# Key preparation in a two-layer attention trunk: layer 0's rotation sums and norm products on VectorE, and the low parts of the keys in one VectorE instruction

## The chip, the cores and the metric

The kernel runs on one core of one Trainium2 chip. The time is the device time of one execution in microseconds (us). In the profile PE is TensorE (matmuls and transposes), PEld its weight loads, DVE is VectorE, ACT is ScalarE, POOL is GpSimd and SP is SyncE, which issues all the large DMAs here.

## The reference, cut to what matters

Two layers act on `x` of 256 tokens by 1024 features. Layer 0 is an attention with 16 query heads in 4 groups: each head attends to compressed keys, to selected blocks of keys (with 256 tokens all blocks are selected) and to a window of keys; three gates mix the results. Layer 1 is a sliding-window attention with 2 key heads and a sink. Both multiply the result with `silu(z)` and project it back.

```python
q = q_groups(rope(rms_norm(split_heads(q, N_HEADS), q_gain), positions), g)
k_slc = kv_groups(rope(rms_norm(split_heads(ks, g), k_gain[1]), positions))   # layer 0
k_win = kv_groups(rope(rms_norm(split_heads(kw, g), k_gain[2]), positions))   # layer 0
k     = kv_groups(rope(rms_norm(split_heads(k, g), k_gain), positions))       # layer 1
```

What matters here is how these keys come about: a head's 64 values are divided by their root mean square, multiplied by a gain, and rotated (`x1*cos - x2*sin`, `x2*cos + x1*sin`).

## The kernel before, in words

All products run in float32 pieces: a value is split into a high part (float32r) and a low part, and a product is made from high times high, high times low and low times high. So each weight tile goes through a copy that rounds it (`wh`, line 141 on ACT, line 143 on DVE) and a subtraction (`wl`, line 169 on DVE) before its matmuls (line 114). Each weight tile's matmuls with `wl` are a third of the tile's matmuls: for a tile of two blocks of 128 rows and both halves of the tokens that is 4 of 12.

The tokens are worked on in two halves of 128 (`h` is 0 or 1), one token per partition. Keys are prepared by `k_prep`, which is called three times: for the window keys of layer 0 (accumulator `akw`), for the selected keys of layer 0 (`aks`), both with 4 key heads (`ng` = 4, so 256 values per token), and for layer 1's keys (`akv`, `ng` = 2, 128 values per token). For each half a call does the following.

- ACT squares the projection (line 310), and DVE sums the squares per head (`kssq`, line 311).
- DVE makes the two rotation terms `t1` and `t2` out of the accumulator (lines 323 and 324); in the trace both are called `rt`.
- POOL turns the sums of squares of both halves into `kr`, one scaling and one power of -0.5.
- POOL adds the rotation terms (`rt<-rt,rt`) and multiplies by the norm (`rt<-rt,kr`).
- ACT writes the high part of the key twice, side by side (`kp<-rt`, line 376).
- The low part is the difference of `t1` and the high part. It is needed twice too: DVE makes copy 0 (line 382), and POOL makes copy 1 (`kp<-rt,kp`, line 66).
- PE transposes the high and the low part (`ptk`, line 385) and ACT copies each to `kt` (line 386).

Every instruction of POOL goes through a small helper class, so POOL's tensor-tensor instructions all stand at line 66 and its tensor-scalar ones at line 71. The tile names tell them apart. `kp` shares its two buffers with `qs`, the split queries, and `ptk` takes one of two PSUM buffers that all transposes share.

The steps of layer 0 are written in the order: window keys, compression (`ph`, `hx`, `kcm`, and on POOL `cssq` and `cr`), selected keys, then queries `q0`, gate `z0`, attention `a0`, queries `q1` and so on. This is not the order in which the instructions run. The framework orders each engine's instructions while it builds the program, by priorities (`tc.high_priority`; `k_prep` has an offset of 250) and by a planner that simulates the engines' times (line 905, `schedule_with_timeline_sim=True`). The result is one fixed list per engine, each worked off in its order. A change of an instruction's engine or size can therefore change the order of others.

The queries of layer 0 (`aq`) use the same accumulators for both of their halves of heads; `q_prep` does for queries what `k_prep` does for keys, with the sum of the rotation terms on POOL (128x512) and the low part on DVE (line 263). The gate `z` is accumulated in a PSUM tile `pz` of which there is one buffer, freed by a DVE product (`zt`, line 400).

Of the kernel before, what the change touches and what calls it, by code (L numbers as in the profile page):

```python
# [20 lines left out]
F32 = mybir.dt.float32  # L21
# [4 lines left out]
ALU = mybir.AluOpType  # L26
# [5 lines left out]
HD = 64  # L32
# [9 lines left out]
PSC1 = 'pp'  # L42
PSL = 'pppd'
SQE = 'aaaa'
RSK, KLO = 'p', 'dp'
OZH, QHI, KHI = 'a', 'a', 'a'
KTM = 'pd'
ZE = 'dp'
OZL, RTE, SSE = 'd', 'p', 'd'
# [41 lines left out]
def tile_hybrid_trunk(ctx: ExitStack, tc: tile.TileContext, x, positions, norm_gains, a_w_in, a_cmp_pos,  # L91
                      a_cmp_w2, a_w_out, b_w_in, b_w_out, small, cmp_w1, out):
    nc = tc.nc
    pool = Pool(nc.gpsimd)
    ENG = {'d': nc.vector, 'p': pool}
# [212 lines left out]
    def sumsq(dst, ps, n, r):  # L308
        sq = work.tile([128, n, HD], F32, name="sq", tag="sq", bufs=1)
        nc.scalar.activation(sq, ps, AF.Square, scale=r)  # L310
        ENG[SSE].tensor_reduce(dst, sq, axis=AX.X, op=ALU.add)

    def rope_terms(ps, n, h, tab, eng='d'):

        t1 = work.tile([128, n, HD], F32, name="rt1", tag="rt1")
        t2 = work.tile([128, n, HD], F32, name="rt2", tag="rt2")
        if tab is None:
            c = trig0[:, h, 2, None, None, :].to_broadcast([128, n, 2, 32])
            s = trig0[:, h, None, 0:2, :].to_broadcast([128, n, 2, 32])
        else:  # L320
            c = halves(tabc[:, h, tab:tab + 1]).to_broadcast([128, n, 2, 32])
            s = halves(tabs[:, h, tab:tab + 1]).to_broadcast([128, n, 2, 32])
        nc.vector.tensor_tensor(halves(t1), halves(ps), c, op=ALU.mult)
        ENG[eng].tensor_tensor(halves(t2), swap_halves(ps, n), s, op=ALU.mult)  # L324
        return t1, t2

    def dup(ap, n):
        return ap[:, :, None, :].to_broadcast([128, n, 2, HD])
# [28 lines left out]
    def k_prep(pss, ng, tab, kt, c0, rf):  # L357

        with tc.high_priority(offset=HPK):
            ssq = work.tile([128, 2, ng], F32, name="kssq", tag="kssq")  # L360
            r = work.tile([128, 2, ng], F32, name="kr", tag="kr")
            for h in range(2):
                sumsq(ssq[:, h], pss[h], ng, rf[:, h:h + 1])
            ts = [rope_terms(pss[h], ng, h, tab, 'd') for h in range(2)]
            pool.tensor_scalar(ssq, ssq, 1.0 / HD, EPS, op0=ALU.mult, op1=ALU.add)
            pool.tensor_tensor(r, ssq, mhalf[:, :, None].to_broadcast([128, 2, ng]), op=ALU.pow)
            for h in range(2):
                t1, t2 = ts[h]
                ENG[RTE].tensor_tensor(t1, t1, t2, op=ALU.add)
                ENG[RSK].tensor_tensor(t1, t1, r[:, h, :, None].to_broadcast([128, ng, HD]), op=ALU.mult)  # L370
                kp = work.tile([128, 2, ng, 2, HD], F32R, name="kp", tag="qs", bufs=NQS)
                for part in range(2):
                    ks = kp[:, part]
                    if part == 0:
                        if KHI == 'a':
                            nc.scalar.activation(ks, dup(t1, ng), AF.Copy)
                        else:
                            for a in range(2):
                                ENG[KHI].tensor_copy(ks[:, :, a], t1)
                    else:  # L380
                        for a in range(2):
                            ENG[KLO[a]].tensor_tensor(ks[:, :, a], t1, kp[:, 0, :, a].bitcast(F32), op=ALU.subtract)
                    pt = ps_t.tile([128, ng, 128], F32R, name="ptk", tag="pt")
                    for g in range(ng):
                        nc.tensor.transpose(pt[:, g], ks[:, g].rearrange("p a d -> p (a d)"), identr)
                    nc.scalar.activation(kt[:, part, :, c0[h]:c0[h] + 128], pt, AF.Copy)
# [200 lines left out]
    with tc.tile_pool(name="cmp", bufs=1) as cp:  # L587
# [20 lines left out]
        for h in range(2):  # L608
# [3 lines left out]
            t1, t2 = rope_terms(kc, 4, h, None, 'd')  # L612
# [18 lines left out]
        def keys_selected():  # L631

            acc = banks("aks", "s")
            for kk in range(4):
                w = load_w(awi, 2 * kk, 2, 1536, 512)
                for h in range(2):
                    proj(acc[h], hT, h, w, 2, 2 * kk)
            k_prep([heads(acc[h][:, 0:256]) for h in range(2)], 4, 2, kt, K_SLC, r0)
            for h in range(2):
                nc.scalar.activation(vv[:, 0, h], acc[h][:, 256:512].rearrange("p (g d) -> p g d", d=HD), AF.Copy,  # L640
                                     scale=r0[:, h:h + 1])

        def keys_window():
            acck = banks("akw")
            for k0 in (0, 4):
                w = load_w(awi, k0, 4, 2048, 256)
                for h in range(2):
                    proj(acck[h][:, 0:256], hT, h, w, 4, k0)
            accv = banks("avw", "s")
            for k0, nk in ((0, 3), (3, 3), (6, 2)):  # L650
                w = load_w(awi, k0, nk, 2304, 304)
                for h in range(2):
                    proj(accv[h][:, 0:304], hT, h, w, nk, k0)
            k_prep([heads(acck[h][:, 0:256]) for h in range(2)], 4, 3, kt, K_WIN, r0)
            for h in range(2):
                nc.scalar.activation(vv[:, 1, h], accv[h][:, 0:256].rearrange("p (g d) -> p g d", d=HD), AF.Copy,
                                     scale=r0[:, h:h + 1])
                gt = work.tile([128, 48], F32, name="gt", tag="gt", bufs=1)
                nc.scalar.activation(gt, accv[h][:, 256:304], AF.Tanh, scale=r0h[:, h:h + 1])
                nc.vector.tensor_scalar(gate[:, h].rearrange("p a b -> p (a b)"), gt, 0.5, 0.5, op0=ALU.mult, op1=ALU.add)  # L660
            nc.vector.tensor_scalar(gate[:, 0, 0, :], gate[:, 0, 0, :], valid, None, op0=ALU.mult)
# [159 lines left out]
    def keys1():  # L821
        acc = banks("akv1", "s")
        wk = [load_w(bwi, k0, 4, 1024, 256) for k0 in (0, 4)]
        for kk in range(2):
            for h in range(2):
                proj(acc[h][:, 0:256], hT, h, wk[kk], 4, 4 * kk)
        k_prep([heads(acc[h][:, 0:128]) for h in range(2)], 2, 5, kt1, (0, 128), r1)
        for h in range(2):
            nc.scalar.activation(v1[:, h], heads(acc[h][:, 128:256]), AF.Copy, scale=r1[:, h:h + 1])
# [79 lines left out]
```

## Time and profile before

| | |
|---|---|
| median of 3 runs | 289.76 us |
| lowest and highest | 289.17 and 291.66 us |
| the profiled execution, its own time | 289.89 us |
| its span, first to last instruction | 288.1 us |
| mean granted TensorE clock | 0.987 of full speed |

The profiled execution's own time is 1.8 us above its span, and 0.13 us above the median. Busy times of an engine are sums over its instructions; instructions of one engine overlap by some hundredths to tenths of a us, so that a row of several together can be shorter than their sum.

### The profile page before, as it was taken

To read this page: it belongs to the slowest core of one execution; us is meant where nothing else is said; L and a number is where in the kernel's file an instruction comes from. 1 tells how busy PE (TensorE), PEld (TensorE's weight loads), DVE (VectorE), ACT (ScalarE), POOL (GpSimd) and SP (SyncE) were. 2 spreads that over 40 slices of the span, in tenths; PEclk is the share of its full clock that TensorE was granted. 3 is DMA by queue.
4 is the path that set the end of the run, shared out by engine and by line. 5 is a ranking of instruction groups with operands and counts; after the bars stand their busy time and mean duration, and the time that the engine had idled before them with its cause. 6 is when DMAs were issued, how large, how long until landed. Compare 5 with 4: busy or idle time off the path is not lost.

```text
span 288.1 us, 5292 instructions
## 1 busy us (share of the span) xinstructions
PE 271.3 (94%) x1772; PEld 229.1 (80%) x1772; DVE 221.1 (77%) x621; ACT 184.2 (64%) x441; POOL 124.3 (43%) x182
## 2 busy tenths in 40 slices
PE   5898999998999799998998999999999799999995
PEld 3667988877898797876776877789989799877874
DVE  3798847579769998988698284989969988784533
ACT  5491974365666767889688473547666949783620
POOL 7494514477720583636252500034394392253200
PEclk9799999999999999999999999999999989999999
DMA  7988769145527544221102354137774423100003
GB/s 224 306 265 262 256 224 245 49 138 147 146 75 200 165 149 146 76 74 36 39 0 75 147 167 127 47 99 220 221 213 154 141 78 104 45 2 0 1 2 146
DMA packets 33115, 37.52 MB, mean 130 GB/s; under 512 B 1680, under 2 KB 21568, under 8 KB 32960
## 3 DMA queue, kind: packets, MB, share of 16 engines
q1 hardware_dynamic: 33088, 37.18, 42.5%
q8 instruction: 14, 0.23, 0.3%
q14 instruction: 13, 0.11, 0.1%
HBM read 36.13 MB, written 1.05 MB: 129 GB/s over the span
## 4 chain that ended last, share of the span: by engine, by line
PE 71%; DVE 15%; ACT 5%; issue 3%; DMA 3%; SPq 1%; POOL 1%; ACTq 0%
PE pz L114 12%; PE po L114 8%; PE aqb L114 7%; PE pyb L114 6%; PE pya L114 6%; PE aq L114 5%; PE ptp L447 5%; DVE wl L169 4%; PE aks L114 4%; DMA wraw<-in_a_w_in_dram 3%; PE s L114 3%; PE avw L114 2%; PE sb L114 2%; DVE p L414 2%; PE akw L114 2%
## 5 line engine op out<-in xcount | busy, mean ns | idle before, releaser
L169 DVE TENSOR_TENSOR wl<-wraw,wh 128x1024 fp32r<-128x1024 f32 (+2 forms) x64 | 79.3, 1245 | 13.6 <-ACT wh L141 12.9
L141 ACT ACTIVATE wh<-wraw 128x1024 fp32r<-128x1024 f32 (+3 forms) x58 | 59.6, 1031 | 29.7 <-PE avw L114 4.9
L114 PE MATMUL pz<-hT,wh 128*128 128x256 f32 x256 | 50.3, 291 | 1.9 <-DVE zt L400 1.9
L114 PEld LDWEIGHTS pz<-hT,wh 128*128 128x128 f32 x256 | 41.4, 194 | 2.2 <-ACT sq L310 2.1
L114 PE MATMUL pz<-hT,wl 128*128 128x256 f32 x128 | 36.8, 287 | 0.0
L71 POOL TENSOR_SCALAR p<-p,rg 128x256 f32<-128x256 f32 (+1 forms) x48 | 22.9, 495 | 29.6 <-DVE rg L768 15.3
L416 ACT ACTIVATE p<-p,nm 128x128 f32<-128x128 f32 (+1 forms) x64 | 28.4, 447 | 4.9 <-DVE nm L414 4.7
L66 POOL TENSOR_TENSOR rt<-rt,rt 128x512 f32<-128x512 f32 (+2 forms) x14 | 21.3, 1530 | 23.8 <-DVE rt L324 23.8
L141 ACT ACTIVATE ptsb<-ptp 128x512 f32<-128x512 f32 x36 | 20.7, 586 | 10.4 <-PE ptp L447 10.4
L114 PEld LDWEIGHTS pz<-hT,wl 128*128 128x128 f32 x128 | 24.8, 194 | 0.0
L414 DVE CUSTOM_DVE_ANT_0 p<-s,mask,nrq 128x128 f32<-128x128 f32 (+1 forms) x64 | 24.2, 407 | 0.0
L114 PE MATMUL aqb<-wh,hT 128*128 128x512 f32 x64 | 21.3, 396 | 0.0
L114 PE MATMUL s<-kt,qT 128*128 128x272 f32 (+1 forms) x96 | 19.6, 305 | 1.6 <-DVE cwide L741 0.7
L114 PE MATMUL aq<-wh,hT 128*128 128x512 f32 x64 | 20.6, 393 | 0.0
L71 POOL TENSOR_SCALAR pb<-pb,rg 128x128 f32<-128x128 f32 (+1 forms) x24 | 13.8, 591 | 15.4 <-DVE rg L865 9.8
L414 DVE CUSTOM_DVE_ANT_0 pb<-sb,mask,nsink 128x128 f32<-128x128 f32 (+1 forms) x32 | 13.8, 471 | 5.1 <-PE ptp L447 3.9
L114 PEld LDWEIGHTS s<-kt,qT 128*128 128x128 f32 x96 | 14.5, 189 | 3.3 <-PE s L114 1.2
L447 PE MATMUL ptp<-identr,p 128*128 128x128 f32 x96 | 15.6, 277 | 1.5 <-ACT ptsb L141 1.4
L416 ACT ACTIVATE pb<-pb,nm 128x128 f32<-128x128 f32 (+1 forms) x32 | 14.2, 446 | 2.6 <-DVE nm L414 2.5
L114 PE MATMUL akc<-wh,hT 128*128 128x512 f32 x32 | 12.3, 451 | 3.0 <-ACT hT L280 1.2
L447 PEld LDWEIGHTS ptp<-identr,p 128*128 128x128 f32 x96 | 11.3, 140 | 3.6 <-ACT ptsb L141 2.1
L114 PEld LDWEIGHTS aq<-wh,hT 128*128 128x128 f32 x64 | 11.9, 188 | 2.5 <-ACT sq L310 0.2
(250 smaller groups left out, 689.5 us busy)
## 6 DMA issues: line engine op xcount, KB each, us to landing
wraw<-in_a_w_in_dram SPq DMA_DIRECT2D x25, 512.0 KB, 4.6
wraw<-in_b_w_in_dram SPq DMA_DIRECT2D x18, 512.0 KB, 4.3
wraw<-in_a_w_out_dram SPq DMA_DIRECT2D x8, 512.0 KB, 3.7
wraw<-in_b_w_out_dram SPq DMA_DIRECT2D x8, 512.0 KB, 4.0
x<-in_x_dram SPq DMA_DIRECT2D x4, 256.0 KB, 3.5
w<-in_cmp_w_dram SPq DMA_DIRECT2D x1, 1024.0 KB, 6.7
x<-in_x_dram SPq DMA_DIRECT2D x2, 512.0 KB, 3.8
wraw<-in_a_w_in_dram SPq DMA_DIRECT2D x2, 456.0 KB, 4.3
```

What stands on the lines that cost most here:

```text
L66: self.eng.tensor_tensor(out, a, b, op=op)
L71: self.eng.tensor_scalar(out, a, s0, s1, op0=op0, op1=op1)
L114: nc.tensor.matmul(o, lhsT=l, rhs=r, start=start, stop=stop)
L141: nc.scalar.activation(dst, src, AF.Copy)
L169: e_.tensor_tensor(wl[:, ks], raw[:, ks], wh[:, ks].bitcast(F32), op=ALU.subtract)
L414: nc.vector.tensor_tensor_reduce(out=p, in0=s, in1=mk, scale=nr, scalar=floor, op0=ALU.add, op1=ALU.min, accum_out=nm)
L416: nc.scalar.activation(p, p, AF.Exp, scale=-1.0, bias=nm, accum_out=total)
L447: nc.tensor.transpose(pt[:, i], s, ident)
```

## The change

In `k_prep` the engine of the rotation sum and of the norm product is now chosen by the number of key heads: VectorE for 4 heads (both calls of layer 0), GpSimd for 2 heads (layer 1), where it was GpSimd for all. The low part's two copies, one by VectorE and one by GpSimd before, are made by a single VectorE instruction that reads `t1` twice through a repeated dimension (`dup`) and writes both copies, in all three calls.

```diff
-RSK, KLO = 'p', 'dp'
+RTK = {4: 'd', 2: 'p'}
...
             for h in range(2):
                 t1, t2 = ts[h]
-                ENG[RTE].tensor_tensor(t1, t1, t2, op=ALU.add)
-                ENG[RSK].tensor_tensor(t1, t1, r[:, h, :, None].to_broadcast([128, ng, HD]), op=ALU.mult)
+                ENG[RTK[ng]].tensor_tensor(t1, t1, t2, op=ALU.add)
+                ENG[RTK[ng]].tensor_tensor(t1, t1, r[:, h, :, None].to_broadcast([128, ng, HD]), op=ALU.mult)
...
                     else:
-                        for a in range(2):
-                            ENG[KLO[a]].tensor_tensor(ks[:, :, a], t1, kp[:, 0, :, a].bitcast(F32), op=ALU.subtract)
+                        nc.vector.tensor_tensor(ks, dup(t1, ng), kp[:, 0].bitcast(F32), op=ALU.subtract)
```

## Rows read from the trace of the kernel before

**Rows 1.** The page's first part: busy time of each engine over the whole span.
```profile
PE 271.3 (94%) x1772; PEld 229.1 (80%) x1772; DVE 221.1 (77%) x621; ACT 184.2 (64%) x441; POOL 124.3 (43%) x182
```
**Rows 2.** PE's waits over the span: waiter, releaser, us in total, times, longest.
```profile
PE sb L114 <- DVE nm L414: 2.0, 1, 2.0
PE pz L114 <- DVE zt L400: 1.9, 1, 1.9
...
PE ptk L385 <- ACT kt L386: 0.7, 1, 0.7
```
**Rows 3.** Busy time in stretches: PE, PEld, DVE, ACT, POOL, granted clock, DMA share, GB/s.
```profile
24.00:98.00 74.00, 73.05 (x494) 64.30 (x494) 56.79 (x122) 43.91 (x82) 36.53 (x33) 1.00 0.58 171
98.00:101.00 3.00, 1.10 (x10) 0.93 (x9) 3.00 (x8) 3.00 (x9) 0.00 (x0) 1.00 0.47 164
49.00:69.00 20.00, 20.00 (x139) 16.66 (x136) 13.85 (x31) 9.69 (x19) 13.37 (x16) 1.00 0.38 107
69.00:78.00 9.00, 8.22 (x56) 7.08 (x55) 8.42 (x14) 5.54 (x9) 6.75 (x5) 1.00 0.67 175
78.00:83.00 5.00, 5.00 (x48) 5.00 (x47) 1.23 (x1) 3.19 (x5) 2.77 (x2) 1.00 0.01 3
83.00:104.00 21.00, 19.10 (x128) 17.51 (x127) 20.90 (x54) 14.07 (x38) 6.59 (x4) 1.00 0.59 176
226.00:232.00 6.00, 4.04 (x24) 3.84 (x24) 6.00 (x15) 5.32 (x20) 3.74 (x3) 0.78 0.30 88
```
**Rows 4.** POOL's groups by shape: busy us, mean ns; idle before and its releaser.
```profile
L66 POOL TENSOR_TENSOR kp<-rt,kp 128x256 fp32r<-128x256 f32 x4 | 5.6, 1394 | 4.1 <-ACT kp L376 4.1
...
L66 POOL TENSOR_TENSOR rt<-rt,rt 128x256 f32<-128x256 f32 x4 | 4.0, 1014 | 2.1 <-DVE rt L324 2.1
...
L66 POOL TENSOR_TENSOR rt<-rt,kr 128x256 f32<-128x256 f32 x4 | 2.4, 613 | 0.1
...
L66 POOL TENSOR_TENSOR kp<-rt,kp 128x128 fp32r<-128x128 f32 x2 | 1.0, 540 | 0.2 <-ACT kp L376 0.2
```
**Rows 5.** POOL in order of time, selected keys: start, us, instruction, idle before.
```profile
60.36 1.65 POOL L66 TENSOR_TENSOR kr<-kssq,mhalf 128x8 f32<-128x8 f32 x1
61.97 1.53 POOL L66 TENSOR_TENSOR rt<-rt,rt 128x256 f32<-128x256 f32 x1
...
67.26 2.84 POOL L66 TENSOR_TENSOR kp<-rt,kp 128x256 fp32r<-128x256 f32 x1 [0.81 <-ACT kp L376]
```
**Rows 6.** DVE in order of time, layer 0's keys and a 128x512 subtraction of layer 1.
```profile
53.84 0.42 DVE L382 TENSOR_TENSOR kp<-rt,kp 128x256 fp32r<-128x256 f32 x1
...
56.09 0.96 DVE L382 TENSOR_TENSOR kp<-rt,kp 128x256 fp32r<-128x256 f32 x1
...
60.23 0.41 DVE L324 TENSOR_TENSOR rt<-aks,tabs 128x256 f32<-128x256 f32 x1
60.56 2.35 DVE L169 TENSOR_TENSOR wl<-wraw,wh 128x1024 fp32r<-128x1024 f32 x2
64.78 0.55 DVE L382 TENSOR_TENSOR kp<-rt,kp 128x256 fp32r<-128x256 f32 x1 [1.87 <-ACT kp L376]
...
205.16 0.68 DVE L263 TENSOR_TENSOR qs<-rt,qs 128x512 fp32r<-128x512 f32 x1
```
**Rows 7.** PE in order of time: queries with low weights, and the last key transposes.
```profile
64.72 0.47 PE L114 MATMUL aq<-wl,hT 128*128 128x512 f32 x1
...
71.82 0.54 PE L385 MATMUL ptk<-identr,kp 128*128 128x128 f32 x4 [0.74 <-ACT kt L386]
```
**Rows 8.** ACT in order of time, ahead of those transposes.
```profile
70.22 1.06 ACT L141 ACTIVATE wh<-wraw 128x1024 fp32r<-128x1024 f32 x1 [3.04 <-PE aq L114]
71.18 0.58 ACT L386 ACTIVATE kt<-ptk 128x512 fp32r<-128x512 f32 x1
```
**Rows 9.** DVE in order of time, layer 1's keys.
```profile
215.33 0.77 DVE L382 TENSOR_TENSOR kp<-rt,kp 128x128 fp32r<-128x128 f32 x2 [2.72 <-ACT kp L376]
216.64 2.36 DVE L169 TENSOR_TENSOR wl<-wraw,wh 128x1024 fp32r<-128x1024 f32 x2 [0.54 <-ACT wh L141]
```

## The prediction, written before the changed kernel was run

> **What bounds the kernel now.** I read the page's busy times first: PE 94%, DVE 77%, POOL 43% [rows 1]. An average hides stages, so I asked next for PE's waits, since only an empty PE can give time back. There are few: the largest are 2.0 us on `nm` in layer 1, 1.9 us on `zt` and 0.7 us on a copy of transposed keys [rows 2]. Then I cut the span into stretches around the edit [rows 3]. From 24 to 98 us PE is busy 73.05 of 74 us, at full clock. Layer 0's two key preparations lie inside, at 49 to 69 us, and there PE is busy all of 20 us, while DVE works 13.85 and POOL 13.37 us. So where the edit is, PE is the bound, and neither engine that trades work is. PE's one hole nearby is in 69 to 78 us, 9.00 - 8.22 = 0.78 us. From 83 to 104 us the second engine is full too: DVE 20.90 of 21 us, and at 98 to 101 us PE loses 1.90 us to it.
>
> The hole at 71 us has a readable cause. PE's last four transposes of high parts wait for a PSUM buffer [rows 7]; ACT frees it by the copy to `kt` at 71.18, but stands in its queue behind a weight copy that started at 70.22 and had waited 3.04 us for PE [rows 8]. ACT was empty before that: had the keys been transposed earlier, the copies would have fitted into the 3.04 us. They came late because the last low part left POOL only at 67.26 + 2.84 = 70.10 us [rows 5].
>
> **What leaves POOL.** In layer 0 four sums, four products and four low copies: 4.0 + 2.4 + 5.6 = 12.0 us; in layer 1 two low copies, 1.0 us [rows 4]. No DMA goes with them. PE never waits on POOL for these directly, so the removal itself is worth nothing; its worth is the earlier date of the keys. The square-root power `kr` stays on POOL and ends at 60.36 + 1.65 = 62.01 us [rows 5].
>
> **What comes to DVE.** A 128x256 subtraction of two SBUF operands takes 0.42 us undisturbed, and a 128x512 one 0.68 us [rows 6]. The sum and the product have the first shape; the product reads one operand repeated, which no row of this size shows from SBUF, so it is bounded by 0.42 and 0.68 and I take 0.42, its size's row. The wide low part reads `t1` repeated and writes both copies; it replaces one 0.42. If the repeat costs nothing it is 0.68; by two old instructions it is 0.84; I take 0.68. Per half: 0.42 + 0.42 + 0.68 - 0.42 = 1.10 us, for four halves 4.4 us (up to 0.26 + 0.16 more in each, 6.1 us). Part comes back at once, because today's low copies are disturbed: the one at 56.09 took 0.96 us and the one at 64.78 took 0.55, against 0.42, together 0.67 us [rows 6]. Net some 3.7 us.
>
> **Its cover.** DVE is idle 20 - 13.85 = 6.15 us from 49 to 69 us [rows 3]; 4.4 fits, and even 6.1 just does. Without that cover it would go straight into DVE's later work.
>
> **The new wait.** The product on DVE now waits for POOL's `kr`. For the selected keys DVE ends the last rotation term at 60.64, and two subtractions of weights stand next in its queue [rows 6]. If sums and products are put ahead of them, DVE does the sums to about 61.4, waits until 62.01, does the products to about 62.8, and the weights begin 2.3 us late. The first would then be ready at 60.56 + 1.18 + 2.3 = 64.0 us. Its user: the twelve matmuls of a query weight tile, of which four take `wl`; counting in fours from the first query matmul, the tile split at 60.56 is first read by PE at 64.72 [rows 7]. That leaves 0.7 us of slack, and the wait costs PE nothing. If both low parts also went in front (two times 0.68 and ACT's high part of 0.63 before them), some 2 us more, PE would be late by about 1.3 us. Between 0 and 1.3 I take 0, since the priorities leave the low parts no reason to pass the weights before ACT has delivered. For the window keys `kr` is done before the rotation terms are, so no wait is added.
>
> **What is early.** With the products done at 62.8, ACT's high parts follow at once, the first some 1 us before today's, and the last low part of the selected keys is due near 66 us in place of 70.10. The transposes can then go before 70 us, and ACT's copies into its idle 3.04 us. This closes the 0.78 us hole at 71. What is late next is the last weight tiles for `aq`, which PE now takes without a wait. A shift of 0.78 us carries through: at 83 us DVE's full stretch begins with work on the gate that PE has just finished, so it moves along, and its 1.90 us loss remains.
>
> **A rule weighed.** POOL's single operations show that the two engines block each other: the low copy at 67.26 took 2.84 us beside DVE's subtractions, and the sum at 61.97 took 1.53 [rows 5], where the mean of the undisturbed products is 0.61 [rows 4]. The Trainium skill, SBUF — State Buffer, section Who interferes with whom, says that a VectorE instruction with two SBUF inputs and a GpSimd instruction that reads SBUF exclude each other for a whole instruction. That speaks for fewer POOL instructions, but against putting DVE work next to POOL's long power. Here the trace differs: the power ran from 60.36 to 62.01, and DVE's two subtractions from 60.56 took 2.35 us together, 1.18 each, no more than elsewhere. By the Trainium skill's rule the sums would be held to 62.01, DVE would lose their 0.8 us more, the first weights would be ready at 64.8, and the total would be 0.1 us above mine. I go by the row.
>
> **Layer 1.** The low parts become two 128x256 instructions of 0.42 in place of two that took 0.77 together [rows 9]: +0.07 us, at most +0.6; a gain is excluded, since PE waits for none of it. After them DVE idles 0.54 us for ACT's weights [rows 9]. I count zero; without that cover the cost is these 0.07 to 0.6 us, since DVE is full from there to 232 us.
>
> **Sum.** 289.89 - 0.78 + 0 + 0 = 289.1 for the profiled execution; it lay 0.13 above the median of the three runs, so I forecast 289.0 us for the median.
>
> **Rivals.**
>
> (a) *Nothing moves.* PE is full at 49 to 69 us, and the fixed list on PE decides when the transposes come. If the planner leaves them at 70 us, the hole stays: 289.8 us. For it: PE's order is set before the run; against: that order comes from planned times, and the planner sees the new engine.
>
> (b) *Faster by more.* The planner's new order lets first scores and gates start earlier on DVE, so that the 1.90 us at 99 us goes too: 289.8 - 0.8 - 1.9 = 287.1. To pass 1% it must also reach layer 1's 2.0 us on `nm` [rows 2], which ends near 229 us, and the low clock behind it: from 226 to 232 us PE worked 4.04 us at a mean granted clock of 0.78 (between the levels of 2.4 and 1.2 GHz) [rows 3], so about 4.04 x 0.22 = 0.9 us of it was lost to the clock. All together: 284.2; half of layer 1's share: 285.7. For it: these are stalls on the order of DVE's queue, which is rearranged; against: both lie 28 and more us behind the edit.
>
> (c) *Slower: DVE becomes the bound.* From 69 to 78 us DVE works 8.42 of 9 us on the queries' rotation and split [rows 3]. If the planner puts key work there rather than into the earlier idle time, the 3.7 us delay the query transposes, and PE, which takes its list in order, waits. The idle 3.77 us of DVE at 78 to 83 us catches part, if PE does not need the queries earlier. It decides from about 2.9 us passed on; the whole price is 289.8 + 3.7 = 293.5.
>
> (d) *The change does not shorten the keys' path*, because `kr` and ACT's queue set it anyway. That gives (a)'s time.
>
> **How the numbers follow.** Chances: the forecast 0.36 (289.0), (a) with (d) 0.24 (289.8), (b) 0.24, (c) 0.16. The first two are within 1% (286.9 to 292.7), which is about what a measurement of this kernel can tell from no change: the runs before spread over 0.9%. (b)'s smaller outcomes near 287 fall at its edge; I count the case as faster because an order that wins one stall tends to be another order everywhere. Range: half of (b) lies above 285.2 and half of (c) below 293.0; cutting there leaves out 0.12 + 0.08. The unknown costs (1.3 for the wait, 1.7 for repeated operands, 0.6 in layer 1, together 3.6 if nothing covers them: 292.6) lie inside.
>
> **What would show it.** Right: no PE wait of `ptk` on `kt`; DVE's wide low part near 0.68 us and its product near 0.42; POOL empty of `rt` work until the queries; the last `ptk` before 72 us; and the full stretch of DVE beginning about 0.8 us sooner than 83 us. Wrong: a DVE wait on `kr` followed by a PE wait on `wl` or `ptq`; DVE above 95% in the stretch of the keys; or a new order in the attention of either layer whose stalls differ by more than all of the above. That order is the weakest point: no row of before shows the planner's new list. By the Trainium skill's rule, sums of DVE beside POOL's power would be stretched beyond 0.42 us.

## The result, and the profile after

The changed kernel took 293.89 us (median of 7 runs, 292.96 to 295.15), the kernel before, on the same chip, 290.87 us (7 runs, 289.17 to 291.98): a ratio of 1.0108, 95% interval 1.0080 to 1.0135. It is slower by 1.1%, and lies outside the range of the prediction (285.2 to 293.0 us). Of the 4.9 us between the forecast of 289.0 and 293.89, 1.1 us is the kernel before itself, whose median is 290.87 in seven runs and was 289.76 in three. The ratios here and below leave out executions that lie over 1.5% above the fastest of their kernel; only e1 has such, three of twelve. The profiled execution took 293.94 us with a span of 292.2 us; before it was 289.89 and 288.1 us.

The moved work did what was wanted of it. Busy times of the engines after, from the page [rows 1]:

```profile
PE 273.7 (94%) x1772; PEld 231.7 (79%) x1772; DVE 226.8 (78%) x629; ACT 185.6 (64%) x441; POOL 110.3 (38%) x168
```

POOL lost 14.0 us and DVE gained 5.7. Busy time in the same stretches as before [rows 3]; the columns are PE, PEld, DVE, ACT, POOL, the granted clock, DMA share and GB/s:

```profile
24.00:98.00 74.00, 73.01 (x491) 63.75 (x490) 58.85 (x123) 42.41 (x74) 24.18 (x21) 1.00 0.59 172
...
49.00:69.00 20.00, 20.00 (x141) 16.66 (x138) 16.72 (x39) 10.04 (x19) 3.10 (x4) 1.00 0.50 135
69.00:78.00 9.00, 8.19 (x50) 6.45 (x49) 8.85 (x12) 5.42 (x10) 4.47 (x2) 1.00 0.44 114
...
83.00:104.00 21.00, 17.89 (x131) 17.22 (x131) 18.50 (x45) 13.23 (x33) 5.16 (x4) 0.94 0.57 176
```

From 49 to 69 us PE is as full as before, though POOL does 10.3 us less there and DVE 2.9 more: the cover was there. Up to 98 us PE has lost nothing. But at 83 to 104 us it does 1.2 us less, and DVE 2.4 us less.

PE's waits after [rows 2], in the columns of before:

```profile
PE pz L114 <- DVE zt L399: 3.1, 1, 3.1
PE sb L114 <- DVE nm L413: 2.0, 1, 2.0
PE s L114 <- DVE nm L413: 1.8, 2, 1.5
...
PE ptkc L697 <- DVE kp L693: 0.8, 1, 0.8
```

The wait of `ptk` on `kt` is gone, and another of 0.8 us stands in its place; the wait on `zt` grew from 1.9 to 3.1, and two waits of scores (`s`) on `nm` of 1.8 together came in, where before there was one of 0.4 us. To see where they lie, three windows that were not cut before; first of the kernel before:

```profile
83.00:98.00 15.00, 15.00 (x96) 13.59 (x95) 14.90 (x41) 9.26 (x25) 4.28 (x2) 1.00 0.63 178
98.00:112.00 14.00, 11.97 (x94) 11.03 (x93) 13.53 (x46) 11.05 (x30) 7.64 (x9) 1.00 0.43 149
120.00:144.00 24.00, 22.25 (x166) 17.60 (x164) 19.22 (x89) 20.20 (x66) 9.47 (x18) 1.00 0.19 61
```

and the same of the changed kernel:

```profile
83.00:98.00 15.00, 15.00 (x116) 14.50 (x116) 12.51 (x33) 8.07 (x18) 3.74 (x2) 1.00 0.60 178
98.00:112.00 14.00, 10.70 (x77) 10.35 (x75) 13.19 (x40) 9.44 (x25) 8.26 (x9) 0.88 0.40 133
120.00:144.00 24.00, 20.94 (x151) 16.98 (x149) 20.91 (x96) 20.90 (x68) 11.12 (x21) 1.00 0.19 57
```

PE loses 11.97 - 10.70 = 1.27 us at 98 to 112 us and 22.25 - 20.94 = 1.31 us at 120 to 144 us, 30 to 75 us behind the edit, and by the lower clock another 10.70 x 0.12 = 1.3 us. Added up that is 3.9 of the 4.1 us between the two spans, an estimate, since each window holds somewhat different work before and after. Dates of both traces say the same: the first product with `vv` of layer 0 (`po`) starts at 115.2 us instead of 112.8, the last at 180.8 instead of 177.0, layer 1's first scores (`sb`) at 225.3 instead of 221.5, the tail's last matmul at 288.4 instead of 284.7. The delay is made by 180 us and only carried after that.

Why there? The instructions of PE are the same 1643 matmuls (the count of the program; the page counts 1772 rows for either kernel), but not in the same order. PE of the kernel before in order of time:

```profile
60.17 0.33 PE L114 MATMUL pk<-w,hx 64*64 64x64 f32 x2
...
70.75 0.33 PE L698 MATMUL ptkc<-identr,kp 64*128 64x64 f32 x2
...
75.76 0.47 PE L114 MATMUL pz<-hT,wh 128*128 128x256 f32 x2
```

and of the changed kernel:

```profile
63.26 0.33 PE L114 MATMUL pk<-w,hx 64*64 64x64 f32 x2
...
70.85 1.00 PE L384 MATMUL ptk<-identr,kp 128*128 128x128 f32 x8
72.66 0.24 PE L697 MATMUL ptkc<-identr,kp 64*128 64x64 f32 x1 [0.81 <-DVE kp L693]
...
77.14 0.24 PE L697 MATMUL ptkc<-identr,kp 64*128 64x64 f32 x1
...
82.19 0.40 PE L114 MATMUL pz<-hT,wh 128*128 128x256 f32 x2
...
101.90 0.76 PE L114 MATMUL pz<-hT,wh 128*128 128x256 f32 x2 [3.10 <-DVE zt L399]
```

The product of the compressed keys, `pk`, comes 3.1 us later than before, and its two transposes `ptkc` stand apart, the second at 77.14 us. `pk` and `ptkc` use the one PSUM buffer of `pz`; the gate's accumulation starts at 82.2 us, not 75.8, the second half's queries go ahead of it, and the first scores come at 88.6 us, not 83.0. A cause for the new list can be argued, and no run shows it: on DVE the compression's `hx`, the input of `pk`, starts at 57.93 us instead of 56.97, behind new work, so a planner that goes by times may see `pk` ready later. On the chip `pk` then stands 5.1 us behind the end of `hx`.

### The profile page after: what moved, and what is told of

Read it like the earlier page. It is cut to its first block, busy times and chain, and to the rows that moved or that the text cites. A ratio compares the mean times of both kernels' runs of the same rounds, so it can differ in the third digit from the quotient of the medians.

```text
span 292.2 us, 5272 instructions
## 1 busy us (share of the span) xinstructions
PE 273.7 (94%) x1772; PEld 231.7 (79%) x1772; DVE 226.8 (78%) x629; ACT 185.6 (64%) x441; POOL 110.3 (38%) x168
## 4 chain that ended last, share of the span: by engine, by line
PE 66%; DVE 17%; POOL 5%; issue 4%; ACT 3%; DMA 3%; SPq 1%; DVEq 0%; POOLq 0%; ACTq 0%
PE pz L114 11%; PE po L114 7%; PE pya L114 7%; PE aq L114 6%; PE pyb L114 6%; DVE wl L169 5%; PE ptp L446 5%; PE aks L114 4%; PE s L114 3%; PE aqb L114 3%; DMA wraw<-in_a_w_in_dram 3%; PE avw L114 2%; PE sb L114 2%; PE akw L114 2%; DVE p L413 2%
## 5 line engine op out<-in xcount | busy, mean ns | idle before, releaser
L169 DVE TENSOR_TENSOR wl<-wraw,wh 128x1024 fp32r<-128x1024 f32 (+2 forms) x64 | 80.9, 1269 | 13.6 <-ACT wh L141 13.0
L114 PE MATMUL pz<-hT,wh 128*128 128x256 f32 x256 | 51.9, 297 | 3.3 <-DVE zt L399 3.1
L114 PEld LDWEIGHTS pz<-hT,wh 128*128 128x128 f32 x256 | 42.7, 200 | 4.3 <-ACT sq L310 3.3
L114 PE MATMUL pz<-hT,wl 128*128 128x256 f32 x128 | 37.7, 294 | 0.0
L71 POOL TENSOR_SCALAR p<-p,rg 128x256 f32<-128x256 f32 (+1 forms) x48 | 24.9, 538 | 32.4 <-DVE rg L767 23.8
L66 POOL TENSOR_TENSOR rt<-rt,rt 128x512 f32<-128x512 f32 (+1 forms) x10 | 16.7, 1676 | 25.9 <-DVE rt L324 20.8
L114 PEld LDWEIGHTS pz<-hT,wl 128*128 128x128 f32 x128 | 25.7, 201 | 0.0
L71 POOL TENSOR_SCALAR pb<-pb,rg 128x128 f32<-128x128 f32 (+1 forms) x24 | 11.3, 488 | 19.7 <-DVE rg L864 14.9
```

Of the source, the lines that this page charges most:

```text
L66: self.eng.tensor_tensor(out, a, b, op=op)
L71: self.eng.tensor_scalar(out, a, s0, s1, op0=op0, op1=op1)
L114: nc.tensor.matmul(o, lhsT=l, rhs=r, start=start, stop=stop)
L169: e_.tensor_tensor(wl[:, ks], raw[:, ks], wh[:, ks].bitcast(F32), op=ALU.subtract)
```

## The experiments

Ratios are to the kernel before, run on the same chip beside each kernel (medians 290.2 to 290.6 us, 17 to 29 runs per set), with the 95% interval.

**TensorE's order forced, in both directions.** The first two kernels change nothing but the order: behind the last instruction, each matmul of PE is made to follow its predecessor in a written list (an order without a semaphore). The planner makes the other engines' lists anew.

```diff
+    PE_ORDER = "0-21 30-31 36-37 ..."     # the other kernel's list
+    for a, b in zip(order, order[1:]):
+        tc.add_manual_dep(pe[b], pe[a].name, NoSync, reason="order")
```

e1, the changed kernel with PE's old list:

> The changed kernel, with TensorE's instructions forced into the order that they have in the kernel before (issue order only, no added waits between engines). Theory 'order': the 1.1% come from the new list on TensorE, which puts layer 0's first scores at 88.6 us in place of 83.0; with the old list the time goes back to that of before or up to 0.8 us below it: ratio 0.996 to 1.002, first scores near 83 us, PE's wait on zt near 1.9 us in place of 3.1. Rival 'DVE load': the loss is the 5.7 us more that DVE is busy; then the order doesn't matter and the ratio stays at 1.008 to 1.014.

e2, the kernel before with PE's new list:

> The kernel before, with TensorE's instructions forced into the order that they have in the changed kernel; the engines of the key preparation are as before. Theory 'order': as slow as the changed kernel, ratio 1.007 to 1.014, first scores near 88 us. Rival 'DVE load': as fast as before, ratio 0.997 to 1.003, since nothing was moved to DVE.

e1 took 1.0078 [1.0042, 1.0114], with a wide spread, 290.4 to 294.4 us in the nine executions counted; e2 took 1.0179 [1.0148, 1.0210], with first scores at 90.0 us. So the new order on PE slows the old work by 1.8%, which speaks for the order; but the old order on PE alone did not bring e1 back: its first scores came at 85.2 us, though the wait on `zt` was the old 1.9 us. The trace of one of its slower executions (293.76 us) shows where that began: ACT's list had been planned anew and put the second `kt` copy ahead of the square of the first queries. PE waited the old 0.74 us for `kt`, then 0.53 us more for that square, and its clock fell. e1's busy time in windows:

```profile
72.00:74.00 2.00, 1.47 (x7) 1.13 (x7) 2.00 (x5) 1.88 (x4) 1.77 (x2) 0.79 0.85 226
74.00:76.00 2.00, 2.00 (x6) 1.54 (x6) 2.00 (x3) 0.69 (x1) 1.05 (x1) 0.50 0.62 156
```

0.50 is the lower of the two levels, 1.2 GHz; in the kernel before, these four microseconds ran at 1.00.

**The shared PSUM buffer taken away.** `pk` and `ptkc` get the tag `pa` in place of `pz`, in the changed kernel (e3) and in the kernel before (e4), so that the gate waits for neither.

```diff
-                pk = ps_a.tile([64, HD], F32, name="pk", tag="pz")
+                pk = ps_a.tile([64, HD], F32, name="pk", tag="pa")
-                pt = ps_a.tile([128, 2, 64], F32R, name="ptkc", tag="pz")
+                pt = ps_a.tile([128, 2, 64], F32R, name="ptkc", tag="pa")
```

> The changed kernel, with two tiles of the compression (the product pk and the transposes ptkc) in the other PSUM buffer (that of ph, pvc and po) in place of the one that the gate's accumulator pz uses. Theory 'pz buffer': the new order comes about because the end of the compression holds pz's buffer until 78.5 us (73.3 before), so that the planner lets the second half of the queries go first; without the sharing pz starts before 76 us and the time is that of before or less: ratio 0.990 to 1.002. Rival: the planner's list differs for another reason, pz comes early and yet the later stalls at 98 to 140 us stay: 1.005 to 1.014.

> The kernel before with the same two tiles moved to the other PSUM buffer. Theory 'pz buffer': here pz started at 75.8 us already, so little is to be gained: ratio 0.992 to 1.003, and the changed kernel with the same move is not slower than this one by more than 0.5%. Rival 'DVE load': the changed kernel with the move stays 1% above this one.

e3 took 1.0125 [1.0091, 1.0160] and e4 1.0080 [1.0051, 1.0109]. With the buffer freed, e3's gate starts at 69.4 us, and nothing is won; and the kernel before loses 0.8% by the move, which takes the sharing with `pz` away and shares the buffer of `ph`, `pvc` and `po` in its place. As a remedy the buffer fell, and e4 shows that a new plan can cost this kernel about what the change cost.

**All five lists kept.** e5 forces PE, ACT, SP and all instructions that POOL and DVE share with the kernel before to the old order; the planner places only the added DVE instructions. e9 forces PE and ACT alone, e10 is the mirror of e5: the old work with all five new lists.

```diff
+    ORDER = {"PE": "...", "Activation": "...", "Pool": "...", "DVE": "...", "SP": "..."}
+    for e, rr in ORDER.items(): ...       # each engine's list as in e1; e9: PE and Activation
```

> The changed kernel, with the lists of all five engines forced to the order of the kernel before (PE, ACT, SP and the instructions that POOL and VectorE still share with it); only the added VectorE instructions (sums, products, wide low parts) are placed by the planner. Theory A (the loss is the planner's new order, on TensorE and on ACT, and nothing of the moved work costs time itself): 0.996 to 1.003 of the kernel before, TensorE's query matmuls of the second half without a fall of the clock at 72 to 78 us, gate accumulation from 76 us and first scores from 83 us, as before the change; the hole of 0.74 us at 71 us stays, since ACT's key copy again stands behind the weight cast. Theory B (the moved work costs time itself, by VectorE's load in 69 to 98 us or by sharing SBUF with POOL): 1.006 to 1.013, with first scores after 85 us though the order is the old one. Theory C (any difference of work shifts some wait and the clock falls): 1.004 to 1.010 with stretches of clock 0.5.

> The changed kernel with the lists of TensorE and ACT forced to those of the kernel before; VectorE, POOL and SP as the planner then places them. With TensorE's list alone forced it took 1.008, with all five 1.001. If ACT's place for the square of the first queries was the rest of it, this is 0.998 to 1.004, with no fall of the clock at 72 to 78 us and first scores from 83 us. If VectorE's or POOL's list carries the rest: 1.005 to 1.009.

> The mirror of the run with all old orders: the kernel before, its work where it was, with the lists of all five engines forced to the order of the changed kernel (POOL's own sums, products and low parts are placed by the planner). Theory A (order is the whole loss): 1.009 to 1.020, at least the loss of the changed kernel, since its lists were made for keys that are ready earlier. Rival (the new lists cost only together with VectorE's added work): 0.998 to 1.004.

| | old lists | new lists |
|---|---|---|
| old work | 1 (the kernel before) | e10: 1.0166 [1.0136, 1.0195] |
| new work | e5: 1.0006 [0.9983, 1.0029] | the change: 1.0108 [1.0080, 1.0135] |

e9 took 1.0010 [0.9989, 1.0031]. This settles the main question. The moved work costs nothing and gains nothing by itself that these runs can tell: 0.1% +- 0.2% with the old lists. The whole loss comes with the new lists. To keep those of PE and ACT is enough: e9 has the old time, with DVE and POOL planned anew around them. Whether DVE's list of the changed kernel costs something of its own is not shown, since e9 does not have it. The forcing itself costs nothing either, unless the moved work gains just as much; no kernel with its own lists forced was run. Under the new lists the new work is even 0.6% faster than the old, as one would expect of lists that were planned for it. And e10 waits where the changed kernel waits, with none of the moved work on DVE:

```profile
PE pz L114 <- DVE zt L400: 3.1, 1, 3.1
...
PE s L114 <- DVE nm L414: 1.8, 2, 1.5
```

In e5's trace DVE has its sums, products and low parts, the first scores are at 83.0 us as before, the wait on `zt` is 1.9 us as before. The 98 to 112 us windows of e5 and of e9, in this order:

```profile
98.00:112.00 14.00, 11.93 (x84) 11.39 (x83) 12.62 (x44) 9.93 (x26) 7.67 (x9) 0.88 0.45 150
```

```profile
98.00:112.00 14.00, 11.98 (x93) 11.03 (x92) 13.53 (x44) 11.06 (x29) 7.64 (x9) 1.00 0.47 150
```

Both have about PE's 11.97 us of before, with the same list. But in e5 the clock fell behind the wait and in e9 it did not. The two microseconds behind the wait, of e5 and of e9:

```profile
102.00:104.00 2.00, 2.00 (x11) 2.00 (x11) 2.00 (x5) 0.88 (x4) 1.92 (x2) 0.50 0.53 190
```

```profile
102.00:104.00 2.00, 2.00 (x19) 2.00 (x19) 2.00 (x6) 1.10 (x4) 1.92 (x2) 1.00 0.66 243
```

From the first scores, at 83.0 us in e5 and before, to the first `po`, e5 loses 1.1 us (113.9 against 112.8). So the 1.3 us of clock in the comparison above need not be the change's own; without them 4.1 us of span become 2.8, near the 3.0 us between the medians. The mean granted clock is 0.990 in the 83 executions of the kernel before that stand beside the experiments, and 0.986 in the changed kernel's seven; whether the new lists also make such falls more frequent stays open.

**The hole at 71 us closed by hand.** e6 is e5 with three of the four last key tiles transposed earlier on PE (in the traces two of them by some 3.5 us, one by 1.7), and on ACT their copies and the square of the first queries moved ahead of the weight copy in which ACT stood waiting [rows 8]. In shorthand, with `aq0` and `aq1` for matmuls of the first queries:

```diff
 PE:   aq0 ... +ptk x8 aq1 ... aq0 ... +ptk x4 aq1 ... -ptk x8 ptkc x2 -ptk x4 aq ...
 ACT:  kp +kt +kt +kt +sq wh -kt -sq -kt qs -kt sq kt
```

> As the one before it, and three of the four key tiles of the second key group are transposed earlier on TensorE (two tiles 3.6 us, one 1.4 us before the end of the first queries), ACT copies them and squares the first queries ahead of the weight cast that it had stood waiting in for 4 us. Theory A: the two holes of TensorE at 71 to 73 us (0.74 and up to 0.53 us) close, so 0.5 to 1.0 us under the run with the old orders, 0.993 to 0.999 of the kernel before; this is the gain that the prediction had counted on (0.78 us). Rival: the 0.78 us come back as another wait (the second queries' weights, cast later by ACT, or the zt wait at 98 us, which grows by as much as TensorE is early), and the time is that of the run with the old orders within 0.2%.

It took 0.9993 [0.9967, 1.0020], 0.1% under e5, not told apart from it, as the rival had it. e6's first two of these transposes in order of time, and its busy time in the stretch:

```profile
66.16 0.46 PE L384 MATMUL ptk<-identr,kp 128*128 128x128 f32 x4
66.91 0.51 PE L384 MATMUL ptk<-identr,kp 128*128 128x128 f32 x4 [0.29 <-DVE kp L381]
```

```profile
69.00:78.00 9.00, 8.90 (x54) 7.41 (x53) 8.40 (x14) 4.56 (x7) 4.76 (x4) 1.00 0.63 160
```

The wait of 0.74 us is gone: PE is busy 8.90 of 9 us, where e5 has 8.22. But 0.29 us came in at 66.9, since the transposes now stand ahead of the date of their low part on DVE, and by 0.2 us this execution was late before the queries. The gate starts at 75.7 us in both, the first scores at 83.0 in both. So the gain that the prediction counted on exists in the stretch, at most some 0.5 us of it, and a measurement of this kernel does not show it.

**The two parts of the change alone, each with the planner's own lists.** e7 has only the wide low parts (`RTK = {4: 'p', 2: 'p'}`); e8 has only the sums and products on DVE:

```diff
-RTK = {4: 'd', 2: 'p'}
+RTK, KLO = {4: 'd', 2: 'p'}, 'dp'
-                        nc.vector.tensor_tensor(ks, dup(t1, ng), kp[:, 0].bitcast(F32), op=ALU.subtract)
+                        for a in range(2):
+                            ENG[KLO[a]].tensor_tensor(ks[:, :, a], t1, kp[:, 0, :, a].bitcast(F32), op=ALU.subtract)
```

> Only the low parts of the keys are changed (one wide VectorE instruction, both layers); sums and products of layer 0 stay on POOL. The planner makes its own list: compression transposes late and gate accumulation after the second half of the queries has begun, as in the changed kernel. Theory A (order): 1.004 to 1.013, first scores after 84 us. Theory B (the moved work itself): a part of 1.1% in proportion to the work moved to VectorE, 0.998 to 1.003, since VectorE gets 0.13 us more per half here and POOL loses 2.8 us per half.

> Only sums and products of layer 0's keys move to VectorE; low parts as before the change (VectorE one copy, POOL the other). The planner's list lies between those of the two kernels (compression transposes between the key tiles, gate accumulation after 8 query matmuls of the second half). Theory A (order): the two parts alone don't add up to the whole; this one 1.002 to 1.010 by where its first scores fall (84 to 87 us). Theory B (the moved work itself): most of the loss, 1.008 to 1.012, with the rest (under 0.003) in the low parts alone.

e7 took 1.0161 [1.0128, 1.0195] and e8 1.0020 [0.9997, 1.0043]. The part with less work added to DVE costs more than the whole, and more than either theory had given it; the other part costs nothing that can be told: 1.6% and 0.2% do not add to 1.1%. (The 2.8 us per half that e7's expectation takes off POOL are those of two halves: four copies took 5.6 us [rows 4].) In e7 PE waits 3.1 us for `nm` in three places, the longest 2.6, and its layer 1 is planned anew too. Costs per instruction would add up; these do not, and the lists differ in each. In e8 the hole at 71 us is gone too, PE is busy 9.00 of 9 us from 69 to 78 us, and again nothing is won.

**Is it the late gate?** The late gate accumulation and scores were my next explanation. e11 and e12 are the changed kernel with one constraint: the second half's query matmuls, from their second step on (e11) or their first (e12), stand behind the first gate accumulation.

```diff
+                if n == 1 and kk == 1:      # e12: kk == 0
+                    after_pe(tc, first matmul of this step, z0_last[0])
```

> The changed kernel with one added constraint and no forced list: the second half's query matmuls from their second step on stand behind the first gate accumulation on TensorE. The planner replans the rest. If the late gate accumulation and the late first scores (88.6 us) are what costs, first scores come before 86 us and the time is 0.998 to 1.006. If any list other than the old one loses as much: 1.008 to 1.016.

> As the run before it, with the constraint on the first step of the second half's query matmuls. If the late first scores are what costs, they come before 84 us and the time is 0.995 to 1.004; if any list other than the old one loses as much: 1.008 to 1.016.

They took 1.0315 [1.0284, 1.0345] and 1.0420 [1.0385, 1.0454], with first scores at 86.9 and 85.8 us: earlier than in the changed kernel, and far slower. Neither outcome had been expected. e12's two longest waits of PE in that stretch, in order of time, and two windows:

```profile
75.03 0.31 PE L709 MATMUL ptkc<-identr,kp 64*128 64x64 f32 x1 [2.29 <-DVE kp L706]
76.80 1.23 PE L358 MATMUL ptq<-identr,qs 128*128 128x128 f32 x8 [1.46 <-DVE qs L271]
```

```profile
69.00:78.00 9.00, 4.45 (x32) 3.58 (x32) 9.00 (x14) 5.75 (x10) 4.45 (x2) 0.79 0.44 117
78.00:83.00 5.00, 5.00 (x34) 5.00 (x34) 0.11 (x1) 1.33 (x4) 3.33 (x3) 0.69 0.00 0
```

The second queries were what kept PE busy while DVE worked on `kp` and `qs`. Without them PE does 4.45 of 9 us, and its clock falls. So in the changed kernel the queries ahead of the gate cover that work. As the planner remade all lists in both kernels, they do not price the late gate alone; they show that early scores are not enough.

**Which stretch of the lists?** e13 has PE's and ACT's old lists up to the last matmul of the second queries (92 us) and the new order behind; e14 the reverse. e15 keeps the new lists, but moves the compression (`pk`, its copies on ACT, the second `ptkc`) to its early place. The code is that of e9, with spliced lists.

> The changed kernel with TensorE's and ACT's lists as in the kernel before up to the last matmul of the second half's queries (92 us), and from there in the order of the changed kernel. Theory H (the loss is made by the head: late gate accumulation, late first scores, VectorE 2.4 us idle in 83 to 98 us and missing from 98 us on): 0.998 to 1.004. Theory T (the loss is made by the order of the attention units behind it): 1.008 to 1.014.

> The reverse: TensorE's and ACT's lists as in the changed kernel up to the last matmul of the second half's queries, and from there in the order of the kernel before. Theory H: 1.008 to 1.015, TensorE waiting at 98 to 102 us over 2.5 us for VectorE. Theory T: 0.998 to 1.004.

> The changed kernel with its own lists of TensorE and ACT, but the compression's product 3 us earlier, at its place in the kernel before, the product's copies on ACT with it, and the second of its transposes directly behind the first; the gate accumulation stays behind the second queries' first steps. If the late compression is the cause: 0.998 to 1.004. If the late gate accumulation and scores are: 1.007 to 1.014, with first scores still after 87 us, and only the 0.8 us wait at 72 us gone.

e13 took 1.0094 [1.0060, 1.0128], e14 1.0062 [1.0038, 1.0086], e15 1.0095 [1.0065, 1.0124]. PE's waits from 96 to 150 us, of e13, e14 and e15 in this order:

```profile
PE ptcs L774 <- DVE cwide L768: 2.1, 1, 2.1
PE pz L114 <- DVE zt L399: 1.9, 1, 1.9
PE s L114 <- DVE nm L413: 1.8, 2, 1.5
```

```profile
PE s L114 <- DVE cwide L740: 2.5, 2, 1.7
PE s L114 <- DVE nm L413: 0.5, 1, 0.5
```

```profile
PE pz L114 <- DVE zt L399: 3.1, 1, 3.1
PE s L114 <- DVE nm L413: 1.8, 2, 1.5
```

e15 has the changed kernel's long waits again and, within the noise, its time, so the late compression does not carry the loss. Its own 0.8 us is not priced by this: the wait of `ptkc` is gone, and 0.7 us of `aq` on ACT's square stand in its place. e13 has the old head, with the first scores at 83.0 us and the old wait on `zt`, and keeps both waits on `nm` of the changed kernel; behind the old head a wait of 2.1 us of `ptcs` on `cwide` comes in as well. e14 has the old tail and no long wait on `zt` or `nm`, but waits 2.5 us on `cwide` instead. Each half of the new lists loses, but 0.9% and 0.6% do not add to 1.1% either: a spliced list is a third list, with waits of its own. The longer waits on `nm` go with the tail; among the kernels made of these two lists, 3.1 us on `zt` come only where the new head and the new tail stand together.

## Why the prediction was wrong, point by point

**The step that failed** is the end of the paragraph "What is early", that "a shift of 0.78 us carries through", and with it the sum, which kept every engine's list of the kernel before behind 78 us. The planner's order was named as the weakest point and as the reason of rival (b), but only with a gain; as a loss it had no price and no share of the range. One of the prediction's own signs of being wrong, a new order in the attention, is what came. It measured +1.0% with the new work (the change against e5) and +1.7% with the old (e10).

**The hole** of 0.78 us. Right: the last keys are early, no `ptk` waits, and the last low part ends at 67.14 + 0.67 = 67.81 us instead of 70.10, though not near 66. Wrong in its worth: the planner's list had a hole of 0.81 us for `ptkc` there, so PE's busy time from 24 to 98 us did not move (73.01 and 73.05). Forced shut in e6 it showed 0.68 us more busy time in its stretch and no difference in the time. DVE's full stretch, due 0.8 us ahead of 83 us, begins at 88.7 us.

**DVE's new work and its cover.** Right. DVE of the changed kernel in order of time [rows 6]:

```profile
49.43 0.75 DVE L369 TENSOR_TENSOR rt<-rt,rt 128x256 f32<-128x256 f32 x2
50.09 0.76 DVE L370 TENSOR_TENSOR rt<-rt,kr 128x256 f32<-128x256 f32 x2
...
59.06 0.42 DVE L369 TENSOR_TENSOR rt<-rt,rt 128x256 f32<-128x256 f32 x1
59.39 1.22 DVE L169 TENSOR_TENSOR wl<-wraw,wh 128x1024 fp32r<-128x1024 f32 x1
...
61.31 0.42 DVE L370 TENSOR_TENSOR rt<-rt,kr 128x256 f32<-128x256 f32 x1
...
63.11 0.69 DVE L381 TENSOR_TENSOR kp<-rt,kp 128x512 fp32r<-128x512 f32 x1
...
71.30 1.30 DVE L693 CAST kp<-kcm 64x128 fp32r<-64x128 f32 x1
...
219.12 0.78 DVE L381 TENSOR_TENSOR kp<-rt,kp 128x256 fp32r<-128x256 f32 x2 [2.72 <-ACT kp L376]
```

Sum and product take 0.42 us, the repeated operand costs nothing, and the wide low part takes 0.69 (0.68 assumed). From 49 to 78 us DVE does 2.87 + 0.43 = 3.3 us more, where a net 3.7 was worked out.

**The new wait** on `kr` costs nothing. `kr` itself came earlier. POOL after, in order of time [rows 5]:

```profile
58.86 1.64 POOL L66 TENSOR_TENSOR kr<-kssq,mhalf 128x8 f32<-128x8 f32 x1
...
70.40 2.13 POOL L66 TENSOR_TENSOR rt<-rt,rt 128x512 f32<-128x512 f32 x1 [3.06 <-DVE rt L324]
```

It ends at 60.50 us, ahead of the first product at 61.31, and DVE has no wait on it.

**The rule weighed.** For the power the row was the better guide again: the sum at 59.06 and the subtraction at 59.39, two SBUF operands each, took their plain 0.42 and 1.22 us, though both began inside the power's 58.86 to 60.50. For another pair the two engines did hold each other: the small rounding copy of the compressed keys took 1.30 us at 71.30, against 0.21 in e5 at 67.58 where POOL ran nothing, and ended at 72.60, with POOL's sum that had started first and ended at 72.53. The Trainium skill, SBUF — State Buffer, section Who interferes with whom, says that a copy or cast on VectorE in its two-port mode and a GpSimd instruction exclude each other, and that the one issued first holds the pair of ports for its whole length; this row agrees with it, though no run shows in which mode the copy ran.

**Layer 1.** Right: two low parts took 0.78 us together (0.77 before), and the delay does not change from 180 us on.

**The rivals.** (a), nothing moves, is what the new work does with the old lists (e5, e9). (b), a new order, did happen, with the other sign. (c) is not what happened: DVE was full at 69 to 78 us (8.85 of 9), but the query transposes made PE wait nowhere, and PE's busy time there is unchanged; its upper end of 293.5 us lies near the result by accident. (d) is out, as the keys' path did get shorter.

**What stays open.** Which of the many exchanges in the lists of PE and ACT cost the time, and whether some list for the new work is faster than the old one: the kernels whose lists the planner made freely took from 1.002 (e8) to 1.042 (e12) of the kernel before, and none was faster. That VectorE's idle 2.4 us at 83 to 98 us is the link between the late scores and the longer wait at 98 us is argued from the windows; no run shows it alone.

## What to carry to other kernels

Where a planner makes the engines' lists, a change of an instruction's engine is two changes, and the second, the new lists, can be the larger. Compare the lists before reading the times, force the old lists on the new work and the new lists on the old, and read the four times as a table: only then is a cost of an instruction told apart from a cost of its order. Before the run, give the new order a term in the sum and a share of the range, as large as what new lists have been seen to move (here losses of 0.2 to 4%, and no gain), however well the stretch with the edit is covered.

## What the runs showed of the hardware that had not been expected

Behind one and the same wait with one and the same list of PE, the granted clock fell in one execution and not in another. Behind the 1.9 us at 98 to 102 us it stayed at 1.00 in e9 and in the kernel before, and fell to 0.50 in e5, which is the lower level of 1.2 GHz; in e5 that cost some 1.1 us by the dates above. Behind layer 1's wait of some 2 us on `nm` it fell in e5 (0.63 at 230 to 234 us) and in the kernel before (0.66), and stayed at 1.00 in e9. In e1 a stretch with two short waits, 0.74 and 0.53 us within two microseconds, was followed by 0.50 too. So a single profile of this kernel carries 1 to 2 us that need not belong to the change, and two spans should be compared window by window with the clock beside them.
